# All modulation sums on VectorE, plain additions for the squares, and loads in long runs, in a decoder layer

## The chip, the core and the metric

The kernel runs on one core of one Trainium2 chip. Its time is device microseconds from the start to the end of one execution; several executions are timed, and one more is recorded by the hardware profiler. TensorE (PE) multiplies matrices at a granted clock of 1.2 or 2.4 GHz, VectorE (DVE) and GpSimd (POOL) work element by element, ScalarE (ACT) applies functions and scales, and SyncE (SP) issues the loads.

## The reference: what is computed

A decoder layer on x of 512 tokens by 2048 channels, all in float32:

```
mod = silu(c) @ w_mod + b_mod            # 2048 x 12288; six rows: sh1 sc1 g1 sh2 sc2 g2
h   = rms_norm(x, ln1_g) * (1 + sc1) + sh1
x   = x + g1 * hybrid_mixer(h)           # w_in (2048 x 3920), w_q_up, two attentions, w_out
h   = rms_norm(x, ln2_g) * (1 + sc2) + sh2
x   = x + g2 * hierarchical_moe(h)       # 32 experts, two per token, three matrices each
```

The mixer has eight heads of sparse attention (an indexer scores the keys, the best 128 are kept) and eight of stick-breaking attention. Of the modulation, c is one vector: silu(c) @ w_mod is a sum of 2048 rows of w_mod, each times one number.

## The kernel before

The program is written out in one order by hand; each engine takes its instructions in that order. All large tiles live in one pool of 23 slots of 8 KB per partition. SyncE issues the loads in the order of a list `items`, three or six items ahead of their use, and a load waits for a free slot.

**Phase one** runs in these stages (times of the profile before). *Start* (0 to 44 us): x arrives transposed in four blocks of 512 channels; ScalarE squares a block, VectorE sums it over its four rows of a partition (line 424, a reduction with a strided view), TensorE sums over the partitions, and `rstd` makes 1/rms. `times_rb` multiplies x by it: the first half of block 0 on VectorE, blocks 2 and 3 on GpSimd (line 430). Then come the tables for the position bias and the masks (lines 442 to 446). *Pieces* (44 to 199): the modulation of h is needed 256 channels at a time. For each of eight pieces `prepare(d)` makes shift and scale, and `piece(d)` projects with the columns of group A and of the first keys (B2). The work of `prepare(d+1)` is interleaved with `piece(d)`. The scale (and in piece 0 the shift too) is summed by TensorE; the shift of the other pieces is summed by `gemv`, 16 calls a piece. *B0 to Q3* (199 to about 350), *Q0, Q1, B1, B3* (to about 520) and *B5* (to 647) are projections of 512 columns in halves; every weight is split by `w_chunk` into a high part (ScalarE) and a low part (line 394, VectorE, or GpSimd from Q0 to B3), since a product takes three matmuls of the parts. Between the matmuls the two attentions are threaded in by `lanes`, four queues of generators that advance at hand-set rates. *O0 to O5* (647 to 897): the output projection in 32 halves; `add_up` multiplies the result by g1 (VectorE) and adds it to x (line 1025, GpSimd for all but the last segment).

The other four rows of the modulation (sc2, g1, sh2, g2; 64 items, 16 chunks of 2048 columns each) are spread among the weights of the later stages: `PRE = 3` first, then `MODS` says how many go into each of the six segments of `SEGS`. A chunk is one call of

```
def gemv(acc, w, s, cut, first):
    lo, hi = slice(0, cut), slice(cut, acc.shape[-1])
    if first:
        V.tensor_scalar(acc[:, lo], w[:, lo], s, None, op0=OP.mult)
        act(acc[:, hi], w[:, hi], AF.Identity, scale=s)
    else:
        V.scalar_tensor_tensor(acc[:, lo], w[:, lo], s, acc[:, lo], op0=OP.mult, op1=OP.add)
        act(w[:, hi], w[:, hi], AF.Identity, scale=s)
        G.tensor_tensor(acc[:, hi], acc[:, hi], w[:, hi], op=OP.add)
```

so VectorE (line 280) takes the columns below `cut` and ScalarE and GpSimd (line 282) the rest: 96 of 256 in the pieces, and of 2048 1280 for sc2 and sh2, 1536 for g1, 768 for g2.

**The experts** (from about 924 us): after a short routing, sixteen pairs of experts, 24 loads of 1 MB each pair, in order; the loads run as far ahead as free slots allow, and the first of them are asked for at the end of phase one.

Of the kernel before, what the change touches and what calls it, by code (L numbers as in the profile page):

```python
# [41 lines left out]
MODS = (5, 7, 4, 11, 4, 30)  # L42
# [4 lines left out]
SHARE = 6  # L47
CUT = (1280, 1280, 1536, 768)
# [29 lines left out]
def tile_hybrid_layer(ctx: ExitStack, tc, A, out, dbg=None):  # L78
    nc = tc.nc
    x, xT, w_mod, w_in, w_q_up, rel_bias, w_out = (  # L80
        A[k] for k in ("x", "xT", "w_mod", "w_in", "w_q_up", "rel_bias", "w_out"))
# [191 lines left out]
    def gemv(acc, w, s, cut, first):  # L273

        lo, hi = slice(0, cut), slice(cut, acc.shape[-1])
        if first:
            V.tensor_scalar(acc[:, lo], w[:, lo], s, None, op0=OP.mult)
            act(acc[:, hi], w[:, hi], AF.Identity, scale=s)
        else:
            V.scalar_tensor_tensor(acc[:, lo], w[:, lo], s, acc[:, lo], op0=OP.mult, op1=OP.add)  # L280
            act(w[:, hi], w[:, hi], AF.Identity, scale=s)
            G.tensor_tensor(acc[:, hi], acc[:, hi], w[:, hi], op=OP.add)  # L282

    def mod_chunk(v, c, q, lag):

        w = raw.pop(("m", v, c, q))
        if c is None:
# [5 lines left out]
            gemv(accs[v], w, sil[:, q:q + 1], CUTS[v], q == 0 and v not in (G1, G2))  # L293
# [8 lines left out]
        for i in range(r):  # L302
# [4 lines left out]
            else:  # L307
                gemv(acc, w[:, i], s, n * SHARE // 16, q == 0 and i == 0)
# [103 lines left out]


# [6 lines left out]
    for c in range(4):  # L420
# [17 lines left out]
    pb = bank("at", "b31")  # L438
    mm(pb[:8, :384], relb, ohd, True, True)
    brow = k2([8, 384], "brow")  # L440
    b31 = sm.tile([8, 1], F32, name="b31")
    V.tensor_copy(b31, pb[:8, 0:1])
    V.tensor_scalar(brow, pb[:8, :384], b31, None, op0=OP.subtract)
    V.tensor_copy(identb, ident)
    V.tensor_scalar(smaskb, ustrict, -NEG, NEG, op0=OP.mult, op1=OP.add)
    V.tensor_scalar(negU, ustrict, -1.0, None, op0=OP.add)
    dram = ctx.enter_context(tc.tile_pool(name="dram", bufs=1, space=bass.MemoryType.DRAM))
    bd = dram.tile([8, 384], F32, name="bd")
    G.dma_start(bd, brow)
# [527 lines left out]
    def main_o(c, q, h, start, stop):  # L977
# [9 lines left out]
        for t in range(4):  # L987
# [568 lines left out]
```

## Time and profile before

| | |
|---|---|
| runs, median of 3 | 1900.78 us (1898.29 to 1902.36) |
| profiled execution, its own time | 1895.36 us |
| its span, first to last instruction | 1893.6 us |
| busy: PE, DVE, ACT, POOL | 1740.0, 973.5, 601.5, 396.2 us |
| mean granted TensorE clock | 0.981 of 2.4 GHz |
| read from HBM | 583.64 MB |

Busy time is summed over the whole span. A matmul's record is longer than its share of PE, so that the PE can be busy throughout and still not at its peak; a wait shorter than that overlap does not show as idle time. The granted clock is a mean over a stretch: 0.5 would be 1.2 GHz throughout.

### The profile page before, as it was taken

The numbers are of one execution on the slowest core, as the hardware profiler recorded it, in microseconds if no ns is written. First come the engines' busy times: TensorE is split into PE (matmuls) and PEld (weight loads), VectorE is DVE, ScalarE is ACT, GpSimd is POOL, SyncE is SP. The second block draws the span as 40 slices with busy tenths as digits, with TensorE's granted clock in tenths as the row PEclk, the third lists the DMA queues.
The fourth block names the chain that finished last, engine by engine and source line by source line (L and its number), as shares of the span: only waits on it lengthen the run. The fifth ranks groups of instructions, "written<-read, shape, count | busy, mean of one in ns | idle before, by whom it ended". The sixth has DMA issues, their size and how long they took to land.

```text
span 1893.6 us, 21355 instructions
## 1 busy us (share of the span) xinstructions
PE 1740.0 (92%) x8097; PEld 976.8 (52%) x8097; DVE 973.5 (51%) x1486; ACT 601.5 (32%) x1136; POOL 396.2 (21%) x311
## 2 busy tenths in 40 slices
PE   4999999998999998899899999999999999999997
PEld 1777777765677676787334333333333333333333
DVE  6888722488855668768334334342433243333325
ACT  3645444554556543443222110111012111211010
POOL 3534311333437326656100000000000000000000
PEclk9999999999999998999999999999999999999999
DMA  9878322323226657768899999999999999999997
GB/s 349 285 263 300 123 79 94 133 90 111 90 89 224 227 178 267 267 245 354 359 418 420 419 420 418 420 419 419 419 420 419 420 419 420 419 420 419 419 413 275
DMA packets 136634, 585.09 MB, mean 309 GB/s; under 512 B 10866, under 2 KB 43802, under 8 KB 79270
## 3 DMA queue, kind: packets, MB, share of 16 engines
q1 hardware_dynamic: 132240, 569.09, 76.6%
q0 software_dynamic: 4288, 14.60, 2.1%
q8 instruction: 65, 1.06, 0.2%
q14 instruction: 41, 0.34, 0.0%
HBM read 583.64 MB, written 8.40 MB: 313 GB/s over the span
## 4 chain that ended last, share of the span: by engine, by line
DMA 39%; PE 20%; DVE 6%; issue 4%; ACT 2%; POOL 1%; SPq 0%; DVEq 0%; POOLq 0%; ACTq 0%
DMA w_u<-in_w_up 15%; DMA w_g<-in_w_gate 12%; DMA w_d<-in_w_down 12%; PE O L103 5%; PE y L103 3%; PE u L103 3%; PE g L103 2%; PE B L103 2%; DVE hl L394 1%; PE cb L103 1%; DVE accv L280 1%; DVE x L1288 1%; PE z L103 1%; PE ga L1252 1%; DMA xg<-x1d,gi 1%
## 5 line engine op out<-in xcount | busy, mean ns | idle before, releaser
L103 PE MATMUL u<-w_u,xe 128*64 128x512 f32 x1024 | 265.8, 605 | 24.4 <-DMA w_u<-in_w_up 23.7
L103 PE MATMUL g<-w_g,xe 128*64 128x512 f32 x1024 | 240.9, 596 | 18.4 <-DMA w_g<-in_w_gate 17.4
L1288 DVE TENSOR_TENSOR x<-cb,x 128x512 f32<-128x512 f32 x256 | 157.3, 682 | 186.7 <-PE cb L103 186.7
L103 PE MATMUL y<-w_d,uT 128*64 128x512 f32 x1024 | 236.9, 600 | 0.7 <-ACT uT L100 0.7
L282 POOL TENSOR_TENSOR accv<-accv,w_m_None 128x768 f32<-128x768 f32 (+2 forms) x62 | 153.0, 2468 | 210.6 <-ACT w_m_None L100 124.0
L1230 POOL DMA_INDIRECT xg<-x1d,gi x15 | 15.2, 1016 | 816.4 <-DVE t L1233 654.9
L103 PEld LDWEIGHTS u<-w_u,xe 128*64 128x64 f32 x1024 | 78.2, 138 | 201.5 <-issue 138.1
L103 PEld LDWEIGHTS g<-w_g,xe 128*64 128x64 f32 x1024 | 76.3, 137 | 170.5 <-issue 129.3
L1278 DVE SCALAR_TENSOR_TENSOR yt<-y,gs,accv 128x512 f32<-128x512 f32 x64 | 47.8, 747 | 200.5 <-PE y L103 200.5
L280 DVE SCALAR_TENSOR_TENSOR accv<-w_m_None,sil,accv 128x1280 f32<-128x1280 f32 (+2 forms) x62 | 132.6, 2138 | 6.2 <-issue 5.5
L100 ACT ACTIVATE xe<-ga,modc 128x128 f32<-128x128 f32 x254 | 94.1, 463 | 128.6 <-PE y L103 88.4
L103 PEld LDWEIGHTS y<-w_d,uT 128*64 128x64 f32 x1024 | 66.6, 136 | 116.1 <-issue 106.7
L100 ACT ACTIVATE uT<-uT 128x512 f32<-128x512 f32 x16 | 9.6, 600 | 343.4 <-PE uT L1329 343.4
L103 PE MATMUL cb<-yH,oT 128*128 128x512 f32 x256 | 107.8, 421 | 0.9 <-DVE x L1288 0.9
L100 ACT ACTIVATE yH<-yt 128x512 fp32r<-128x512 f32 x64 | 40.3, 630 | 204.5 <-DVE yt L1278 121.4
L103 PE MATMUL cb<-yL,oT 128*128 128x512 f32 x256 | 101.1, 395 | 0.0
L1280 DVE TENSOR_TENSOR yL<-yt,yH 128x512 fp32r<-128x512 f32 x64 | 44.3, 693 | 110.3 <-PE g L103 63.2
L394 DVE TENSOR_TENSOR hl<-w_O,hl 128x1024 fp32r<-128x1024 f32 x32 | 67.8, 2123 | 40.1 <-ACT hl L100 31.2
L282 POOL TENSOR_TENSOR acc<-acc,w_m 128x160 f32<-128x160 f32 x105 | 61.3, 584 | 70.1 <-ACT w_m L100 62.4
L103 PEld LDWEIGHTS cb<-yH,oT 128*128 128x128 f32 x256 | 48.0, 188 | 49.6 <-issue 38.6
L1252 PEld LDWEIGHTS ga<-cst,xg 128*128 128x128 f32 x252 | 35.2, 209 | 61.8 <-issue 41.0
L1323 DVE TENSOR_TENSOR u<-sg,u 128x512 f32<-128x512 f32 x16 | 11.0, 689 | 105.4 <-PE u L103 105.4
(435 smaller groups left out, 3171.5 us busy)
## 6 DMA issues: line engine op xcount, KB each, us to landing
w_g<-in_w_gate SPq DMA_DIRECT2D x128, 1024.0 KB, 19.9
w_u<-in_w_up SPq DMA_DIRECT2D x128, 1024.0 KB, 21.2
w_d<-in_w_down SPq DMA_DIRECT2D x128, 1024.0 KB, 19.9
w_m_None<-in_w_mod SPq DMA_DIRECT2D x64, 1024.0 KB, 5.0
w_m<-in_w_mod SPq DMA_DIRECT2D x32, 1024.0 KB, 11.0
w_B<-in_w_in SPq DMA_DIRECT2D x48, 512.0 KB, 4.7
w_O<-in_w_out SPq DMA_DIRECT2D x16, 1024.0 KB, 5.9
w_A<-in_w_in SPq DMA_DIRECT2D x8, 848.0 KB, 11.7
```

What stands on the lines that cost most here:

```text
L100: return SC.activation(o, i, f, **kw)
L103: return T.matmul(o, l, r, start=start, stop=stop, skip_group_check=skip)
L280: V.scalar_tensor_tensor(acc[:, lo], w[:, lo], s, acc[:, lo], op0=OP.mult, op1=OP.add)
L282: G.tensor_tensor(acc[:, hi], acc[:, hi], w[:, hi], op=OP.add)
L394: low_eng[0].tensor_tensor(t[:, 1], s, t[:, 0].bitcast(F32), op=OP.subtract)
L1230: G.indirect_dma_start(xs, None, x1d[:, :], bass.IndirectOffsetOnAxis(ap=gi[:, 0:1], axis=0), bounds_check=S - 1, oob_is_err=False)
L1252: T.transpose(pb[:, 128 * j:128 * j + 128], xs[:, 512 * c:512 * c + 512].rearrange("p (k j) -> p j k", j=4)[:, j], ident)
L1278: V.scalar_tensor_tensor(yt, y, g, rowv[G2][:, cs], op0=OP.mult, op1=OP.mult)
L1280: V.tensor_tensor(yL[:, cs], yt, yH[:, cs].bitcast(F32), op=OP.subtract)
L1288: return lambda: V.tensor_tensor(acc[q][:, t], pb, acc[q][:, t], op=OP.add)
L1323: V.tensor_tensor(u, sg, pb, op=OP.mult)
```

## The change

`gemv` loses its cut: one VectorE instruction takes all columns, and neither ScalarE nor GpSimd has a part. `times_rb` runs on VectorE for all blocks: half of block 0 at once, its other half before piece 0, and blocks 1, 2 and 3 after the pieces 0, 2 and 4. The squares of a block are summed by two additions. The masks and the bias row, with their matmul and a store, go ahead of the squares. The four chunks of piece 0's modulation are loaded two ahead of the first weights and two behind, not all behind. `MODS` is new, and `add_up` works on VectorE alone. On the host, the weights of phase one (the first two rows of w_mod, w_in, w_q_up, w_out) and x are laid out so that a load reads one run of 4 to 8 KB for each partition, where it read runs of 1 to 4 KB; the bytes loaded are the same.

```diff
-MODS = (5, 7, 4, 11, 4, 30)
+MODS = (20, 2, 6, 12, 4, 17)
-SHARE = 6
-CUT = (1280, 1280, 1536, 768)
...
             o, n, r = PIECES[c]
-            return w_mod_v[:, r * q:r * q + r, v * D + o:v * D + o + n], [P, r, n]
+            return A["w_m1"][c, v, q].rearrange("p (r n) -> p r n", r=r), [P, r, n]
...
-            return w_in_v[c][:, h, :, 0:NA], [P, 2, NA]
+            return A["w_a"][c, h].rearrange("p (j n) -> p j n", j=2), [P, 2, NA]
...
-            return w_in_v[c][..., BCOL + 512 * n:BCOL + 512 * (n + 1)], [P, 2, 2, 512]
+            return A["w_b"][n, c].rearrange("e p (j n) -> p e j n", j=2), [P, 2, 2, 512]
...
-            return w_o_v[:, 4 * q:4 * q + 4, 512 * c:512 * (c + 1)], [P, 4, 512]
+            return A["w_o"][c, q].rearrange("p (j n) -> p j n", j=4), [P, 4, 512]
...
-        k = len(mod) // 2 if d else 0
+        k = len(mod) // 2
         items += mod[:k] + wa + mod[k:] + wb
...
-    def gemv(acc, w, s, cut, first):
+    def gemv(acc, w, s, first):
         if first:
-            V.tensor_scalar(acc[:, lo], w[:, lo], s, None, op0=OP.mult)
-            act(acc[:, hi], w[:, hi], AF.Identity, scale=s)
+            V.tensor_scalar(acc, w, s, None, op0=OP.mult)
         else:
-            V.scalar_tensor_tensor(acc[:, lo], w[:, lo], s, acc[:, lo], op0=OP.mult, op1=OP.add)
-            act(w[:, hi], w[:, hi], AF.Identity, scale=s)
-            G.tensor_tensor(acc[:, hi], acc[:, hi], w[:, hi], op=OP.add)
+            V.scalar_tensor_tensor(acc, w, s, acc, op0=OP.mult, op1=OP.add)
...
-        V.tensor_reduce(sr, sq.rearrange("p j t -> p t j"), axis=AX.X, op=OP.add)
+        V.tensor_tensor(sq[:, 0:2], sq[:, 0:2], sq[:, 2:4], op=OP.add)
+        V.tensor_tensor(sr, sq[:, 0], sq[:, 1], op=OP.add)
         mm(pss, ones, sr, c == 0, c == 3)
...
     times_rb(0, range(2), V)
-    for c in (2, 3):
-        times_rb(c, range(4), G)
...
     times_rb(0, range(2, 4), V)
-    times_rb(1, range(4), V)
     for d in range(len(PIECES)):
...
+        if d in (0, 2, 4):
+            times_rb(d // 2 + 1, range(4), V)
...
-        eng.tensor_tensor(x1[c][:, t], x1[c][:, t], tmp, op=OP.add)
+        V.tensor_tensor(x1[c][:, t], x1[c][:, t], tmp, op=OP.add)
```

## Rows read from the trace of the kernel before

**Rows 1.** The page's chain that ended last, shares of the span by line.
```profile
DMA w_u<-in_w_up 15%; DMA w_g<-in_w_gate 12%; DMA w_d<-in_w_down 12%; PE O L103 5%; PE y L103 3%; PE u L103 3%; PE g L103 2%; PE B L103 2%; DVE hl L394 1%; PE cb L103 1%; DVE accv L280 1%; DVE x L1288 1%; PE z L103 1%; PE ga L1252 1%; DMA xg<-x1d,gi 1%
```

**Rows 2.** Windows cut at the stages; columns as in the heading line.
```profile
core 0: us, PE busy (x) PEld busy (x) DVE busy (x) ACT busy (x) POOL busy (x), PEclk, DMA share, GB/s
0.00:44.00 44.00, 18.07 (x79) 5.57 (x79) 30.09 (x28) 14.29 (x14) 14.91 (x16) 0.94 1.01 349
44.00:199.00 155.00, 146.01 (x974) 114.19 (x975) 137.04 (x232) 89.43 (x182) 69.08 (x109) 0.98 0.81 274
199.00:387.00 188.00, 184.03 (x804) 137.44 (x803) 75.78 (x92) 89.32 (x148) 47.27 (x38) 1.00 0.30 101
387.00:520.00 133.00, 119.61 (x548) 82.80 (x547) 115.32 (x240) 69.70 (x150) 45.95 (x22) 0.94 0.31 103
520.00:647.00 127.00, 120.45 (x573) 89.35 (x571) 76.11 (x80) 75.75 (x138) 61.26 (x41) 0.99 0.45 163
647.00:720.00 73.00, 65.47 (x263) 48.24 (x262) 48.60 (x46) 32.38 (x48) 27.14 (x19) 0.99 0.54 194
720.00:897.00 177.00, 162.42 (x894) 135.79 (x894) 135.92 (x82) 70.16 (x96) 110.80 (x51) 0.94 0.79 292
897.00:924.00 27.00, 18.14 (x98) 11.10 (x99) 13.87 (x67) 5.62 (x16) 2.11 (x2) 0.87 0.83 341
924.00:1893.00 969.00, 905.77 (x3876) 352.30 (x3872) 340.73 (x623) 154.90 (x350) 17.65 (x17) 0.99 1.00 411
```

**Rows 3.** What PE waited for from 44 to 199 us: total, times, longest.
```profile
PE B L103 <- DVE attA L484: 6.7, 6, 1.3
PE sh L103 <- DVE acc L280: 2.3, 1, 2.3
```

**Rows 4.** What PE waited for from 720 to 897 us.
```profile
PE O L103 <- DVE hl L394: 16.0, 4, 6.2
```

**Rows 5.** Timeline of the start: start, us, engine, line, instruction.
```profile
9.27 14.38 DVE L424 TENSOR_REDUCE sqr<-xsq 128x512 f32<-128x2048 f32 x4 [5.52 <-ACT xsq L100]
...
15.20 1.91 ACT L100 ACTIVATE xsq<-xt 128x2048 f32<-128x2048 f32 x1 [0.59 <-DMA xt<-in_xT]
...
23.71 2.08 PE L103 MATMUL xss<-sqr,one 128*128 128x512 f32 x2 [1.46 <-DVE sqr L424]
...
27.08 3.64 PE L103 MATMUL md<-w_m,sil 128*32 128x256 f32 x32
...
43.94 0.79 PE L103 MATMUL cq<-h0H,waH 128*128 128x512 f32 x1 [7.43 <-ACT h0H L100]
```

**Rows 6.** Timeline of VectorE: single modulation sums.
```profile
343.21 1.54 DVE L280 SCALAR_TENSOR_TENSOR accv<-w_m_None,sil,accv 128x1280 f32<-128x1280 f32 x1
...
865.70 3.67 DVE L280 SCALAR_TENSOR_TENSOR accv<-w_m_None,sil,accv 128x768 f32<-128x768 f32 x1
...
880.68 1.01 DVE L280 SCALAR_TENSOR_TENSOR accv<-w_m_None,sil,accv 128x768 f32<-128x768 f32 x1
```

**Rows 7.** VectorE's groups by shape from 44 to 199 us.
```profile
L280 DVE SCALAR_TENSOR_TENSOR acc<-w_m,sil,acc 128x96 f32<-128x96 f32 x105 | 54.5, 519 | 3.7
```

**Rows 8.** Line 394's instructions: least, median and largest ns.
```profile
L394 DVE TENSOR_TENSOR hl<-w_O,hl x32: 1211/2076/3960, 647.0 to 881.6; 128x1024 fp32r<-128x1024 f32 x32
...
L394 POOL TENSOR_TENSOR hl<-w_B,hl x17: 2365/2389/3900, 384.1 to 569.3; 128x1024 fp32r<-128x1024 f32 x17
```

**Rows 9.** Line 1025's instructions: least, median and largest ns.
```profile
L1025 DVE TENSOR_TENSOR x<-x,mix x4: 691/692/693, 888.5 to 895.0; 128x512 f32<-128x512 f32 x4
```

**Rows 10.** A window while x arrives; columns as in rows 2.
```profile
10.00:15.00 5.00, 2.01 (x2) 0.50 (x2) 5.00 (x2) 3.82 (x2) 0.00 (x0) 1.00 1.02 405
```

**Rows 11.** VectorE's groups by shape from 387 to 520 us.
```profile
L280 DVE SCALAR_TENSOR_TENSOR accv<-w_m_None,sil,accv 128x1280 f32<-128x1280 f32 x6 | 11.8, 1973 | 0.0
```

**Rows 12.** VectorE's groups by shape from 720 to 897 us.
```profile
L280 DVE SCALAR_TENSOR_TENSOR accv<-w_m_None,sil,accv 128x768 f32<-128x768 f32 x16 | 35.4, 2210 | 5.6 <-issue 5.5
L280 DVE SCALAR_TENSOR_TENSOR accv<-w_m_None,sil,accv 128x1280 f32<-128x1280 f32 x13 | 30.2, 2321 | 0.1
```

**Rows 13.** SyncE's queue from 866 us: the first expert load.
```profile
869.83 4.65 SPq L256 DMA_DIRECT2D w_g<-in_w_gate  x4
```

More of the change, by code (lines that the diff above doesn't have):

```diff
@@ L79, in tile_hybrid_layer @@
     nc = tc.nc
-    x, xT, w_mod, w_in, w_q_up, rel_bias, w_out = (
-        A[k] for k in ("x", "xT", "w_mod", "w_in", "w_q_up", "rel_bias", "w_out"))
+    xT, w_mod, rel_bias = (A[k] for k in ("xT", "w_mod", "rel_bias"))
     w_gate, w_up, w_down = A["w_gate"], A["w_up"], A["w_down"]
@@ L292, in mod_chunk @@
                     G.dma_start(accs[v][0:1], A["b_gate"][int(v == G2):int(v == G2) + 1])
-            gemv(accs[v], w, sil[:, q:q + 1], CUTS[v], q == 0 and v not in (G1, G2))
+            gemv(accs[v], w, sil[:, q:q + 1], q == 0 and v not in (G1, G2))
             if q == 15:
@@ L307, in mod_chunk @@
             else:
-                gemv(acc, w[:, i], s, n * SHARE // 16, q == 0 and i == 0)
+                gemv(acc, w[:, i], s, q == 0 and i == 0)
     def first_cols(c):
@@ L411, in advance @@
         load_to(n_done + AHEAD)
+    V.tensor_copy(identb, ident)
+    V.tensor_scalar(smaskb, ustrict, -NEG, NEG, op0=OP.mult, op1=OP.add)
+    V.tensor_scalar(negU, ustrict, -1.0, None, op0=OP.add)
+    pb = bank("at", "b31")
+    mm(pb[:8, :384], relb, ohd, True, True)
+    brow = k2([8, 384], "brow")
+    b31 = sm.tile([8, 1], F32, name="b31")
+    V.tensor_copy(b31, pb[:8, 0:1])
+    V.tensor_scalar(brow, pb[:8, :384], b31, None, op0=OP.subtract)
+    dram = ctx.enter_context(tc.tile_pool(name="dram", bufs=1, space=bass.MemoryType.DRAM))
+    bd = dram.tile([8, 384], F32, name="bd")
+    G.dma_start(bd, brow)
     rb = sm.tile([P, S], F32, name="rb", tag="rb", bufs=2)
@@ L432, in tile_hybrid_layer @@
     times_rb(0, range(2), V)
-    for c in (2, 3):
-        times_rb(c, range(4), G)
[L438 to L449, printed above, removed]
     tb = []
@@ L982, in main_o @@
             xc = slot([P, 4, 512], name=f"x1_{c}")
-            Q.dma_start(xc, x_v[:, :, 512 * c:512 * c + 512])
+            Q.dma_start(xc, A["x"][c].rearrange("p (t d) -> p t d", t=4))
             x1.append(xc)
@@ L995, in main_o @@
             if (c, q, h) == (3, 3, 1):
-                add_up(c, t, pm, V)
+                add_up(c, t, pm)
                 keep(c, t)
@@ L1013, in main_o @@
                 for t in range(4):
-                    add_up(c, t, pm, G)
+                    add_up(c, t, pm)
                 if q == 3:
@@ L1532, in _prepare @@
     cst, ohd, flip = _constants()
+    w_in = f("w_in")[0]
     a = {
-        "x": f("x").reshape(512, 2048), "xT": f("x").reshape(512, 2048).T, "w_mod": f("w_mod")[0],
-        "w_in": f("w_in")[0], "w_q_up": f("w_q_up")[0], "rel_bias": f("rel_bias"),
-        "w_out": f("w_out")[0], "w_gate": f("w_gate")[0], "w_up": f("w_up")[0], "w_down": f("w_down")[0],
+        "x": f("x").reshape(4, 128, 4, 512).transpose(2, 1, 0, 3).reshape(4, 128, 2048),
+        "xT": f("x").reshape(512, 2048).T, "w_mod": f("w_mod")[0],
+        "w_m1": f("w_mod")[0, :, :4096].reshape(128, 2, 8, 2, 8, 256).transpose(4, 3, 1, 0, 2, 5).reshape(8, 2, 2, 128, 2048),
+        "w_a": w_in[:, :NA].reshape(4, 2, 128, 2 * NA),
+        "w_b": w_in[:, NA:].reshape(4, 2, 128, 2, 6, 512).transpose(4, 0, 1, 2, 3, 5).reshape(6, 4, 2, 128, 1024),
+        "w_q": f("w_q_up")[0].reshape(4, 128, 4, 512).transpose(2, 1, 0, 3).reshape(4, 128, 2048),
+        "w_o": f("w_out")[0].reshape(4, 4, 128, 4, 512).transpose(3, 0, 2, 1, 4).reshape(4, 4, 128, 2048),
+        "rel_bias": f("rel_bias"), "w_gate": f("w_gate")[0], "w_up": f("w_up")[0], "w_down": f("w_down")[0],
         "router": fold(np.concatenate([f("router_g")[0], f("router_e")[0]], axis=1)), "vecs": vecs, "b_gate": bm[[2, 5]], "cst": cst, "ohd": ohd, "flip": flip,
```

11 lines of the change are left out of this document (2 added, 9 removed).

## The prediction

> **What bounds the kernel now.** First the chain that ended last [rows 1]: the loads of the experts' three matrices hold 15 + 12 + 12 = 39% of the span in it. Next the windows, cut at the stages [rows 2]: from 924 to 1893 us the loads move 411 GB/s at a DMA share of 1.00. So the expert part is a load stream of fixed length, and what comes before matters only through the time at which that stream can start. Before 897 us the loads are not the limit, except in the first 44 us (share 1.01). PE is: it is busy 184.0 of the 188 us from 199 to 387. So the change can win only where PE waits or is slowed before 897 us. That room, from rows 2 (window minus PE busy, plus what the clock costs: one minus the granted clock, times the window) is: 44 to 199, 9.0 + 3.1; 199 to 387, 4.0; 387 to 520, 13.4 + 8.0; 520 to 647, 6.5 + 1.3; 647 to 720, 7.5 + 0.7; 720 to 897, 14.6 + 10.6. The view of PE's waits names the culprits: in 44 to 199 VectorE's additions and sums [rows 3], in 720 to 897 VectorE's halves of the output weights, 16.0 us in four waits [rows 4]. And PE has no projection matmul to do before 43.94 us [rows 5].
>
> **Price of one instruction.** A modulation sum alone costs VectorE 1.54 us for 1280 columns and 1.01 us for 768 [rows 6], so 1.04 ns a column: 2048 columns are 1.54 + 768 × 0.00104 = 2.34 us, and 256 columns 1.01 − 512 × 0.00104 = 0.48 us (estimates from these two rows). Beside GpSimd the same 768 columns took 3.67 us [rows 6], and the 96-column sums average 519 ns [rows 7], more than 256 columns alone would. The halves of the output weights go from 1.21 us at best to 2.08 in the median [rows 8]. So with GpSimd's share moved onto VectorE, VectorE's total becomes about equal, not larger.
>
> **The start.** The last square ends at 15.20 + 1.91 = 17.1 us, the last reduction at 9.27 + 14.38 = 23.65, and the last sum matmul starts at 23.71 [rows 5]. Two plain additions, 1024 and 512 wide, cost 1.21 [rows 8] + 0.69 [rows 9] = 1.9 us, so that matmul starts at 19.0: 4.7 us sooner. The masks, now ahead of the squares, wait for small constants; VectorE has nothing to do before 9.27 us, which hides them. Were the constants as late as the last square, the masks' 4 us (estimate: five small instructions under 1 us each) would go in front of the additions; I price them at nothing. PE then runs the shift sums from 21.1 to 24.7 (3.64 us [rows 5]), a turn of 1 us, and the scale sums to 29.4. Before, the same order ended at 35.5, and another 8.4 us passed to the first projection matmul, with VectorE in a weight half and in tiny additions beside GpSimd's x products. Without those I estimate that tail as copy 0.4, turn 0.5, three small operations 0.5, scale 0.8, cast 0.6: 2.9 us. First projection matmul at 29.4 + 2.9 = 32.3, **11.5 us** sooner. Do the loads keep up? It needs 9.7 MB (x 4.2, constants 0.4, first weights 0.9, four sums 4.2); about 5.0 MB are in at 15 us. At the 349 GB/s of the first 44 us [rows 2], mostly runs of 1 KB, the rest is there at 28.5; at the 405 of x's longer runs [rows 10] at 26.6. The last scale sums start at 27.6. So the new layout is worth about 1 us here, and nothing in the pieces, which load at 274 GB/s [rows 2]. Bounds for the start: 4.7 (the squares alone) to 13.
>
> **The pieces (44 to 199).** PE waits about 1.1 us in each of six pieces, and 2.3 in the first [rows 3]. VectorE's sums of one piece go from 16 × 0.52 = 8.3 to 16 × 0.48 = 7.7 us; with its other work freed of GpSimd I take 1.4 us less in all. But the x products of the next 512 channels (4 × 0.69 = 2.8 us) now stand in front of the sums in pieces 1, 3 and 5: there VectorE is 1.4 us later than before and the wait grows from 1.1 to 2.5; in pieces 2, 4 and 6 it goes; the first loses its 2.3. Sum: −2.3 − 3 × 1.1 + 3 × 1.4 = −1.4; with less slow clock at the beginning **2 us** gained (bounds: 3 lost, 9 gained).
>
> **The middle.** Twenty sums now lie in 199 to 350 where five lay: 15 × 2.34 = 35 us more on a VectorE that is busy 76 of 188 [rows 2], hidden by PE's projections. Each may delay a half a little: I take 3 us lost, against 2 gained at the bias table, whose flip matrix is asked for once GpSimd's additions before it are done: **−1**. In 387 to 520, where VectorE is busy 115 of 133, eight sums of 2.34 stand for seven of about 2.0 [rows 11], 5 us more; GpSimd's sums no longer stand in VectorE's way there, for which I take 6 back: **+1**. In 520 to 647 twelve for eleven, **+1**. Bounds of the three: 15 lost, 25 gained.
>
> **The output projection.** 647 to 720 keeps four sums; the normalisation that ends in it loses GpSimd's additions as neighbours, they cost VectorE 0.69 each [rows 9]: **+4** of the room of 8. In 720 to 897 the sums fall from 30 to 17: 40 us in place of 66 [rows 12]; 24 halves cost 29 us at 1.21 in place of 50 at 2.08; sixteen gated additions in two steps 22. VectorE is left with about 95 of some 155 us instead of 136 of 177. The four waits for halves should go, and with them most of the slow clock of that stretch: **+20** of the 25 (bounds 8 and 25).
>
> **Sum.** 11.5 + 2 − 1 + 1 + 1 + 4 + 20 = 38.5 us. The expert stream begins with a load at 869.83 us [rows 13], asked for three items ahead of the projections' end; with a shorter tail it gains a little less, but in 897 to 924 the share is 0.83 [rows 2], which takes some of that up: I charge 1.5. The profiled execution took 1895.4 us; 1895.4 − 37 = 1858. It lies 5.4 under the runs' median of 1900.8, so against the runs: **1863 us**.
>
> **A rule against it.** Rows 6 show GpSimd and VectorE stretching each other. GpSimd keeps weight halves, 2.39 us each in the median [rows 8], in the stretch from 350 to 570, and the stick additions. The Trainium skill (SBUF — State Buffer, "Who interferes with whom") says that a VectorE instruction with two SBUF inputs and a GpSimd one that reads SBUF exclude each other for the whole instruction. The trace agrees in kind: 3.67 us are far more than a shared rate would make of 1.01. By that rule a longer sum means a longer block on both sides; what it would cost here is rival (c).
>
> **Rivals.**
> (a) All the room is won: 11.5 + 12.1 + 4 + 21.4 + 7.8 + 8.2 + 25.2 = 90, so about 1811. For it: the waits named have VectorE as their releaser. Against: in 387 to 520 its load does not fall. Chance 0.15.
> (b) The wait moves to 199 to 350. In 720 to 897, at 1.25 sums a half, PE lost 16.0 us over 24 halves [rows 4], 0.67 each; at one sum a half over 20 halves that is 13 us: 1876. Against: VectorE was busy 77% there and will be at some 60% here. Chance 0.16.
> (c) GpSimd's remaining halves and the longer sums block each other from 387 to 520: eight sums, each lengthened by one half of 2.39, are 19 us on the busiest VectorE: 1882. Against: GpSimd's own sums, which met them before, are gone. Chance 0.12.
> (d) The other side: in 199 to 350 the weight loads come late, since every second item is now a sum and only three items are loaded ahead. Twenty halves in 150 us are 7.5 us each; three items are a half and a half, 11 us, plus the half that is split ahead. A stall above 37 / 20 = 1.9 us a half decides for slower; at 3 us it is 1863 + 60 = 1923. Against: the DMA share there is 0.30 [rows 2], and 15 MB more at 400 GB/s add 37 of 188 us, 0.2. Chance 0.09.
>
> **Numbers.** The forecast 1863 (its own range 1845 to 1872) has 0.48, the rivals 0.15, 0.16, 0.12, 0.09. Leaving out half of (a) and all of (d) gives the range 1830 to 1886. A difference under 0.2% (3.8 us) can't be told from none. Faster: 0.48 + 0.15 + 0.16 + 0.11 = 0.90; same 0.03; slower 0.07, mostly (d).
>
> **What would show it.** First projection matmul near 32 us; no wait of PE for VectorE's halves in the last stage before the experts; sums of 2048 columns at 2.3 us each; the first expert load near 833 us, and the expert part as long as before. Wrong would be: waits for weight halves between 199 and 350, a start later than 38 us, or projections that end earlier without an earlier first expert load.

## The result and the profile after

| | before | after |
|---|---|---|
| runs, median of 4 | 1900.62 us (1898.29 to 1902.36) | 1875.8 us (1875.28 to 1876.9) |
| profiled execution, its own time | 1895.36 us | 1876.25 us |
| its span | 1893.6 us | 1874.4 us |
| busy: PE, DVE, ACT, POOL | 1740.0, 973.5, 601.5, 396.2 us | 1735.2, 938.9, 507.6, 153.2 us |

The ratio is 0.9877 (0.9863 to 0.989): the kernel is 1.2% faster, 24.8 us between the medians and 19.1 between the two profiled executions, on which all the sums below are made. (The kernel before ran 2.9 us faster in its profiled execution than in the fastest of its timed runs, which is most of the difference of the two figures.) A gain of 37 us was forecast: the direction is right and 1875.8 lies in the range of 1830 to 1886, but half of the gain is missing from the profile.

The chain that ended last, by line:
```profile
DMA w_u<-in_w_up 15%; DMA w_g<-in_w_gate 12%; DMA w_d<-in_w_down 12%; PE O L100 8%; PE B L100 7%; PE y L100 3%; PE u L100 3%; PE Q L100 2%; PE g L100 2%; PE z L100 2%; DVE accv L269 2%; DVE acc L269 1%; PE cb L100 1%; DVE sel L722 1%; DMA w_m<-in_w_m 1%
```
It answers to [rows 1]. The experts' loads hold the same 39%; in what stands before them PE's projections grew (`O` from 5 to 8%, `B` from 2 to 7%), and VectorE's halves are no longer listed.

Windows, cut where PE's work stands at the stages' boundaries (271 and 331 are added cuts inside B0 to Q3):
```profile
core 0: us, PE busy (x) PEld busy (x) DVE busy (x) ACT busy (x) POOL busy (x), PEclk, DMA share, GB/s
0.00:32.40 32.40, 14.90 (x78) 4.74 (x78) 15.91 (x31) 14.18 (x14) 2.51 (x8) 0.89 0.96 378
32.40:190.60 158.20, 149.54 (x976) 116.79 (x976) 136.51 (x239) 50.44 (x66) 6.72 (x3) 0.96 0.75 296
190.60:271.00 80.40, 77.35 (x327) 59.79 (x326) 54.93 (x54) 32.70 (x52) 8.92 (x10) 0.98 0.58 208
271.00:331.00 60.00, 49.41 (x304) 35.93 (x303) 22.29 (x23) 15.60 (x25) 5.95 (x6) 0.91 0.39 137
331.00:398.00 67.00, 66.78 (x307) 48.13 (x306) 28.57 (x45) 36.73 (x69) 20.16 (x15) 1.00 0.29 98
398.00:527.60 129.60, 114.95 (x487) 80.22 (x486) 114.24 (x232) 62.83 (x142) 32.81 (x14) 0.96 0.26 90
...
720.00:879.70 159.70, 154.33 (x890) 130.73 (x890) 87.47 (x81) 39.88 (x69) 6.83 (x9) 0.99 0.70 264
...
905.00:1874.00 969.00, 905.75 (x3870) 351.55 (x3866) 340.65 (x623) 153.32 (x347) 17.59 (x17) 0.99 1.00 411
```
They answer to [rows 2]. The expert part is 969 us at 411 GB/s, as before to the digit. The stage to look at is 271 to 331: PE idles 10.6 of 60 us, where it was idle for 4.0 us in all of 199 to 387 [rows 2], and in that stretch VectorE too is busy for only 22.29 us, ScalarE for 15.60. All are waiting for something.

To see where the time went, take the start of the same projection matmul in two timelines and subtract. Counted are the matmuls that write `cq`, `B`, `Q` and `O`, 2304 in every kernel, in order of time. The table, worked out from the timelines, holds microseconds earlier than before; the other columns are kernels of the next section.

| matmul, its time before | after | old_mods | held_slot | twelve | shared_sums | best4 |
|---|---|---|---|---|---|---|
| 1st, 43.94 | 11.5 | 12.6 | 11.2 | 12.7 | 12.5 | 10.6 |
| 384th, 198.88 (end of the pieces) | 8.7 | 9.2 | 7.2 | 9.5 | 4.2 | 10.1 |
| 672nd, 286.43 | 7.0 | 12.4 | 10.3 | 11.6 | 2.9 | 13.3 |
| 768th, 313.93 | -8.5 | 12.3 | 4.7 | 4.8 | 2.9 | 13.3 |
| 960th, 386.53 | -10.0 | 12.3 | 4.7 | 4.1 | 2.9 | 10.1 |
| 1248th, 527.19 | -6.0 | 10.9 | 1.5 | 14.7 | -0.5 | 15.8 |
| 1536th, 643.83 | -5.1 | 15.2 | 5.9 | 19.1 | -1.2 | 18.1 |
| 2304th, 893.72 (the last) | 16.8 | 38.6 | 28.7 | 44.1 | -0.9 | 42.0 |

Each column is one execution, and two executions of one kernel differ by some us: the 1st matmul, up to which old_mods, held_slot, twelve, shared_sums and best4 do the same work as after, starts between 10.6 and 12.7 us early.

The start came out as forecast. Timeline of the start:
```profile
16.19 1.91 ACT L97 ACTIVATE xsq<-xt 128x2048 f32<-128x2048 f32 x1 [0.76 <-DMA xt<-in_xT]
...
18.14 1.23 DVE L426 TENSOR_TENSOR xsq<-xsq 128x1024 f32<-128x1024 f32 x1 [0.71 <-ACT xsq L97]
...
19.47 0.69 DVE L427 TENSOR_TENSOR sqr<-xsq 128x512 f32<-128x512 f32 x1
...
20.21 2.08 PE L100 MATMUL xss<-sqr,one 128*128 128x512 f32 x2 [1.61 <-DVE sqr L427]
...
32.44 0.50 PE L100 MATMUL cq<-h0H,waH 128*128 128x512 f32 x1 [2.23 <-ACT h0H L97]
```
They answer to [rows 5]: the last sum matmul starts 2.1 us after the last square, the two additions last 1.23 and 0.69, and the first projection matmul is at 32.44 where 32.3 was forecast.

The tail too. PE's waits from 720 to 880 us, total, times, longest:
```profile
PE router L100 <- DVE router L963: 3.4, 1, 3.4
PE O L100 <- DVE mix L1013: 1.0, 1, 1.0
PE O L100 <- DVE hl L381: 0.8, 1, 0.8
```
Of the 16.0 us for halves [rows 4] 0.8 are left. The durations behind it, least, median and largest ns (line 269 is the sum, 381 the half):
```profile
L269 DVE SCALAR_TENSOR_TENSOR acc<-w_m,sil,acc x105: 483/485/491, 37.5 to 165.0; 128x256 f32<-128x256 f32 x105
L269 DVE SCALAR_TENSOR_TENSOR accv<-w_m_None,sil,accv x62: 2330/2344/3815, 177.8 to 852.5; 128x2048 f32<-128x2048 f32 x62
...
L381 DVE TENSOR_TENSOR hl<-w_O,hl x32: 1215/1222/1482, 650.9 to 851.3; 128x1024 fp32r<-128x1024 f32 x32
```
The prices 0.48 and 2.34 us for the sums were right, and the halves of the output weights went from a median of 2.08 [rows 8] to 1.22.

What was lost, from 190 to 331 us, stands in the waits; ScalarE's helper is line 97, its `hl` is the high half of a weight:
```profile
ACT hl L97 <- DVE accv L269: 29.0, 7, 9.4
...
ACT hl L97 <- PE B L100: 11.0, 3, 8.3
ACT hl L97 <- PE md L100: 10.5, 1, 10.5
...
PE z L100 <- DVE st L803: 6.4, 2, 3.8
ACT hl L97 <- PE pob L100: 4.7, 1, 4.7
```
A high half reads only a loaded weight. It has no data from a modulation sum (`accv`), from a projection's matmul (`B`, or the attention's `pob`) or from the matmuls that turn a finished modulation row into columns (`md`). What it does need is a slot of the pool for its result, and what it waits for is the last user of the tile that had the slot before. The timeline of all engines shows what stands behind it:
```profile
278.13 0.62 ACT L97 ACTIVATE st<-st,one 128x384 f32<-128x384 f32 x1
...
281.63 19.79 SPq L247 DMA_DIRECT2D w_m_None<-in_w_mod  x2
...
287.04 1.06 ACT L97 ACTIVATE hl<-w_B 128x1024 fp32r<-128x1024 f32 x1 [8.29 <-PE B L100]
288.00 0.85 ACT L97 ACTIVATE st<-z 128x384 f32<-128x384 f32 x2
...
290.79 1.19 PE L100 MATMUL z<-st,mone 128*128 128x256 f32 x2 [3.79 <-DVE st L803]
...
297.10 2.35 DVE L269 SCALAR_TENSOR_TENSOR accv<-w_m_None,sil,accv 128x2048 f32<-128x2048 f32 x1 [6.46 <-DMA accv<-in_b_gate]
299.49 1.06 ACT L97 ACTIVATE hl<-w_B 128x1024 fp32r<-128x1024 f32 x1 [9.44 <-DVE accv L269]
300.45 0.96 ACT L97 ACTIVATE st<-z 128x384 f32<-128x384 f32 x2
```
ScalarE stops for 8.29 us at the high half. The next instructions in its order are those of the stick attention (`st<-z`); they come 0.96 us after the half starts, VectorE's `st` after them, and PE, which has the attention's matmul `z` next in its order, has been idle for 3.79 us by then. The two load issues from 281.63 us, spread over 19.79 us, point to the same shortage at SyncE.

### The profile page after: what moved, and what is told of

The parts are those of the page before. It is cut to its first block, busy times and chain, and to the rows that moved or that the text cites. A ratio compares the mean times of both kernels' runs of the same rounds, so it can differ in the third digit from the quotient of the medians.

```text
span 1874.4 us, 20840 instructions
## 1 busy us (share of the span) xinstructions
PE 1735.2 (93%) x8097; PEld 975.6 (52%) x8097; DVE 938.9 (50%) x1518; ACT 507.6 (27%) x960; POOL 153.2 (8%) x116
## 4 chain that ended last, share of the span: by engine, by line
DMA 41%; PE 36%; DVE 14%; issue 4%; ACT 4%; POOL 1%; SPq 0%; DVEq 0%; ACTq 0%; POOLq 0%
DMA w_u<-in_w_up 15%; DMA w_g<-in_w_gate 12%; DMA w_d<-in_w_down 12%; PE O L100 8%; PE B L100 7%; PE y L100 3%; PE u L100 3%; PE Q L100 2%; PE g L100 2%; PE z L100 2%; DVE accv L269 2%; DVE acc L269 1%; PE cb L100 1%; DVE sel L722 1%; DMA w_m<-in_w_m 1%
## 5 line engine op out<-in xcount | busy, mean ns | idle before, releaser
L269 DVE SCALAR_TENSOR_TENSOR accv<-w_m_None,sil,accv 128x2048 f32<-128x2048 f32 x62 | 150.4, 2426 | 6.7 <-DMA accv<-in_b_gate 6.5
L1219 POOL DMA_INDIRECT xg<-x1d,gi x15 | 15.2, 1014 | 818.7 <-DVE t L1222 597.2
L97 ACT ACTIVATE hl<-w_B 128x1024 fp32r<-128x1024 f32 x48 | 50.5, 1052 | 54.9 <-DVE accv L269 29.5
L381 DVE TENSOR_TENSOR hl<-w_O,hl 128x1024 fp32r<-128x1024 f32 x32 | 39.2, 1229 | 43.6 <-ACT hl L97 28.3
L381 POOL TENSOR_TENSOR hl<-w_B,hl 128x1024 fp32r<-128x1024 f32 x17 | 47.9, 2817 | 142.6 <-ACT hl L97 112.3
## 6 DMA issues: line engine op xcount, KB each, us to landing
w_u<-in_w_up SPq DMA_DIRECT2D x128, 1024.0 KB, 21.2
```

The source lines that it names most:

```text
L97: return SC.activation(o, i, f, **kw)
L269: V.scalar_tensor_tensor(acc, w, s, acc, op0=OP.mult, op1=OP.add)
L381: low_eng[0].tensor_tensor(t[:, 1], s, t[:, 0].bitcast(F32), op=OP.subtract)
L1219: G.indirect_dma_start(xs, None, x1d[:, :], bass.IndirectOffsetOnAxis(ap=gi[:, 0:1], axis=0), bounds_check=S - 1, oob_is_err=False)
```

## Experiments

Four theories stood for the 15 us lost between 271 and 331 us. **S**: the 23 slots run out, because a loaded chunk of 8 KB now stands beside every half; the high half waits for a slot and holds back ScalarE's queue. **V**: VectorE's twenty longer sums delay the halves, as rival (b) had it. **G**: the gates' bias row does it, since the first sum of g1 waits for a memset on GpSimd and a load, 6.46 us above. **L**: the loads come late, as in rival (d). Diffs are against the kernel after; times are medians, ratios are to the kernel before on the same chip.

| kernel | us (lowest to highest) | ratio (95%) |
|---|---|---|
| old_mods | 1859.6 (1858.55 to 1860.19) | 0.9793 (0.9777 to 0.9809) |
| ahead2 | 1874.21 (1869.88 to 1875.46) | 0.9866 (0.9848 to 0.9883) |
| no_gate_row | 1882.83 (1880.14 to 1885.09) | 0.992 (0.9904 to 0.9937) |
| twelve | 1854.68 (1851.05 to 1860.67) | 0.9778 (0.9757 to 0.98) |
| held_slot | 1865.52 (1862.62 to 1867.38) | 0.9821 (0.9806 to 0.9836) |
| shared_sums | 1898.14 (1893.24 to 1903.33) | 0.9995 (0.9984 to 1.0007) |
| old_squares | 1881.83 (1880.99 to 1887.29) | 0.992 (0.9901 to 0.9939) |
| old_layout | 1861.77 (1861.26 to 1866.32) | 0.9811 (0.9793 to 0.983) |
| spread_rb | 1877.04 (1870.18 to 1879.88) | 0.988 (0.9854 to 0.9906) |
| best2 | 1857.42 (1856.6 to 1859.7) | 0.9784 (0.9771 to 0.9798) |
| best3 | 1852.34 (1850.53 to 1853.78) | 0.9756 (0.9743 to 0.9769) |
| best4 | 1851.21 (1849.14 to 1853.91) | 0.9747 (0.9734 to 0.9761) |

### The respread undone: old_mods

```diff
-MODS = (20, 2, 6, 12, 4, 17)
+MODS = (5, 7, 4, 11, 4, 30)
```


> The changed kernel with the old spread of the sums (5, 7, 4, 11, 4, 30). Theory S (the 23 slots run out in 271 to 331 us, since one loaded chunk now stands beside every weight half): the idle and slow PE of that stretch (10.6 us idle, about 5 us of slow clock) goes; the output projection carries 30 sums of 2.34 us, 70 + 29 + 22 = 121 of some 160 us of VectorE, and loses at most 8 us of its gain; about 1868 us. Rival V (it is VectorE's long sums that delay PE, wherever they stand): the output projection loses most of its 19 us again; 1880 us or more.

Measured 1859.6, 16 us less than after. The windows and the first waits from 190 to 331 us:
```profile
190.00:271.00 81.00, 81.00 (x347) 62.39 (x346) 37.52 (x46) 33.15 (x53) 4.17 (x9) 1.00 0.30 103
271.00:331.00 60.00, 58.99 (x253) 44.34 (x251) 14.46 (x15) 27.57 (x44) 8.99 (x10) 1.00 0.26 91
```
```profile
ACT hl L97 <- DVE accv L269: 5.4, 2, 3.3
ACT hl L97 <- PE B L100: 3.1, 3, 1.1
```
So the respread alone made the loss. And it bought nothing: with thirty sums instead of seventeen in O2 to O5, the stretch from 641 us to the last matmul gains 38.6 − 15.2 = 23.4 us (last two rows of the table), against 16.8 + 5.1 = 21.9 after. The measurement is below what either theory gave, since the tail lost nothing. Whether the chunks' storage or their sums made the loss is not told by this run, as it takes both away.

### Fewer loads ahead: ahead2

```diff
+    AHEAD = 2
     steps("B0", 0.5)
...
+    AHEAD = 3
     low_eng[0] = G
```


> The changed kernel, but from B0 to Q3 loads are asked for two items ahead, not three; sums and their places are the same. Theory S (slots): one slot fewer is held by loaded data, so PE's idle time from 271 to 331 us falls from 10.6 to under 5 us; about 1868 us. Rival V (VectorE's sums): unchanged, 1876. Rival L (the loads come late): the waits for weight halves grow, over 20 us idle there, 1885 or more.

Measured 1874.21, hardly less than after. In the window from 271 to 331 us PE is busy 54.23 us, against 49.41 after, so its idle time falls from 10.6 to 5.8. Its row:
```profile
271.00:331.00 60.00, 54.23 (x333) 39.72 (x331) 22.98 (x25) 20.54 (x33) 8.55 (x8) 0.94 0.45 158
```
That a shorter lookahead helps here speaks for S and against L. But S had asked for under 5 us and a total of 1868, and got neither; the total is nearer to V's 1876, and by the ratios it can't be told from after. ScalarE's halves wait elsewhere instead: for `B` 24.2 us in four waits from 190 to 331 us, the longest 10.8.

### Without the gates' bias row: no_gate_row

The kernel leaves out the bias of the two gates.
```diff
-                if v in (G1, G2):
-                    G.memset(accs[v], 0.0)
-                    G.dma_start(accs[v][0:1], A["b_gate"][int(v == G2):int(v == G2) + 1])
-            gemv(accs[v], w, sil[:, q:q + 1], q == 0 and v not in (G1, G2))
+            gemv(accs[v], w, sil[:, q:q + 1], q == 0)
```


> The changed kernel with its new spread, but the gate accumulators (g1, g2) start with a plain product like the others: no GpSimd memset, no load of the bias row, no wait of VectorE for it. It leaves the gates' bias out. Theory G (the loss in 271 to 331 us comes from the start of g1's accumulator, which now falls among the stick additions: VectorE stood 6.5 us before that load): PE's idle time there falls from 10.6 to under 4 us; about 1866. Theory S (no free slot, whatever starts): it stays above 8 us; 1872 or more.

Measured 1882.83: slower than after, not faster. Its row of that window:
```profile
271.00:331.00 60.00, 47.82 (x287) 34.36 (x286) 20.28 (x22) 13.73 (x22) 3.84 (x4) 0.86 0.36 123
```
PE idles 12.2 us. The wait for the bias row was a consequence that happened to be in the same place: GpSimd's memset at 292.96 had stood behind the stick attention's additions, which were late already. G is out. Why this kernel is 7 us slower than after is not shown.

### Twelve chunks in the first segment: twelve

```diff
-MODS = (20, 2, 6, 12, 4, 17)
+MODS = (12, 0, 4, 11, 4, 30)
```


> The changed kernel with MODS (12, 0, 4, 11, 4, 30): against the old spread only seven chunks move from Q0, Q1 and B1 into the first segment, and g1's accumulator starts in the same place as with the old spread. Theory G (start of the gate accumulator): nothing is lost in the first segment, 1859 like the old spread. Theory S (loaded chunks hold the slots): about half of the 16 us is lost there, 1867.

Measured 1854.68. Its row of that window:
```profile
271.00:331.00 60.00, 54.71 (x224) 41.01 (x223) 16.50 (x13) 22.00 (x37) 6.63 (x8) 0.94 0.31 106
```
Both expected totals, 1859 and 1867, were missed. Twelve chunks idle PE for 5.3 us, between the 1.0 of five and the 10.6 of twenty, and the table shows 6.7 us lost between the 672nd and the 768th matmul (15.5 after). The wait of 8.3 us on `B` is there again, at 282.46 us, and PE's 3.8 on `st` with it. From the 960th to the 1248th matmul it wins 10.6 where old_mods loses 1.4: there the seven chunks of the second segment (Q0, Q1, B1) are gone, and best2, which has none there either, wins 11.8. This brings the total below both expectations; the prediction too had weighed longer sums against shorter ones there, and not a stretch without any. (The profiled execution of twelve is the fastest of its runs, 3.6 us under their median.)

### One slot fewer, and nothing else: held_slot

old_mods, and an empty tile that holds one slot of the pool through B4. No load and no sum is added, two memsets of one column on GpSimd take it and free it.
```diff
-MODS = (20, 2, 6, 12, 4, 17)
+MODS = (5, 7, 4, 11, 4, 30)
...
+    held = [slot([P, D], name=f"held{k}") for k in range(1)]
+    for t in held:
+        G.memset(t[:, 0:1], 0.0)
     steps("B4", RATES[0])
+    for t in held:
+        G.memset(t[:, 0:1], 1.0)
     steps("Q2", RATES[0])
```


> The changed kernel with the old spread of the sums and one slot of the pool held by an empty tile throughout B4: no more loads and no more sums than with the old spread. Theory S (free slots): the projections lose time there as they do with twenty chunks, 3 to 10 us between 199 and 331 us, ScalarE's high halves waiting for slots; 1863 to 1870. Rival V (VectorE's sums or the loads themselves are what delays): nothing is lost, 1859.6 within 2 us.

Measured 1865.52, 5.9 more than old_mods and within the expected 1863 to 1870; the ranges of the two kernels do not meet, the intervals of their ratios just touch. In the table it loses 5.6 us between the 672nd and the 768th matmul, where old_mods loses none. The window of 271 to 331, and the timeline:
```profile
271.00:331.00 60.00, 55.42 (x233) 41.78 (x232) 11.98 (x11) 23.01 (x38) 5.97 (x9) 0.97 0.25 88
```
```profile
283.68 1.06 ACT L97 ACTIVATE hl<-w_B 128x1024 fp32r<-128x1024 f32 x1 [8.29 <-PE B L100]
...
287.44 0.67 PE L100 MATMUL z<-st,mone 128*128 128x256 f32 x2 [3.79 <-DVE st L803]
...
289.09 0.10 POOL L928 MEMSET held<- 128x1 f32 x1
289.22 1.06 ACT L97 ACTIVATE hl<-w_B 128x1024 fp32r<-128x1024 f32 x1 [2.52 <-POOL held L928]
```
With VectorE at 11.98 us of 60, less than in any of the others, the loss is back, down to the same 8.29 and 3.79 us. The last line says it in one row: a high half of a weight waits 2.52 us for a memset of a tile with which it has nothing in common but the slot. So one slot fewer is enough for this loss, without one sum or load more: S is shown, and V is not needed for it.

How the 16 us of after divide is not shown. Its twenty chunks hold slots as loaded data, but they also bring the end of sc2 and the beginning of g1 into this stretch: 3 + 20 chunks are sixteen of sc2 and seven of g1, so that two accumulators of a slot each stand side by side. The wait of 10.5 us is for `md`, the last reader of sc2's accumulator, and the sum at 297.10 is the first of g1. In twelve, where g1 starts later, 6.7 us are lost where after loses 15.5. Nor does the trace list which slots are free at a moment: that they are short is read from the waits.

### Sums shared as before: shared_sums

old_mods, with the sums again cut among VectorE, ScalarE and GpSimd; all else as after.
```diff
-MODS = (20, 2, 6, 12, 4, 17)
+MODS = (5, 7, 4, 11, 4, 30)
...
+    CUTS = {SC2: 1280, SH2: 1280, G1: 1536, G2: 768}
...
+        lo, hi = slice(0, cut), slice(cut, acc.shape[-1])
...
+            V.scalar_tensor_tensor(acc[:, lo], w[:, lo], s, acc[:, lo], op0=OP.mult, op1=OP.add)
+            act(w[:, hi], w[:, hi], AF.Identity, scale=s)
+            G.tensor_tensor(acc[:, hi], acc[:, hi], w[:, hi], op=OP.add)
```


> The changed kernel with the old spread and the old sharing of the sums between VectorE, ScalarE and GpSimd. If GpSimd's share stretched VectorE and made the halves late, the output projection loses its 19 us again and the pieces and the middle some 3 to 6: about 1883 against 1859.6 with all sums on VectorE. Rival (the sharing was harmless, what helped in the output projection were the gated additions on VectorE): 1866 or less.

Measured 1898.14, no different from before (0.9984 to 1.0007), and 38.5 more than old_mods; 1883 was expected. All the other edits together are worth nothing without this one: the 12.5 us of the start are there in the table, and gone at the 1248th matmul. The costliest groups of the page show the exchange, here of shared_sums (busy us, mean ns, then idle before):
```profile
L275 POOL TENSOR_TENSOR accv<-accv,w_m_None 128x768 f32<-128x768 f32 (+2 forms) x62 | 153.8, 2481 | 249.4 <-ACT w_m_None L97 153.6
...
L273 DVE SCALAR_TENSOR_TENSOR accv<-w_m_None,sil,accv 128x1280 f32<-128x1280 f32 (+2 forms) x62 | 130.9, 2111 | 6.6 <-issue 5.1
```
and of old_mods:
```profile
L269 DVE SCALAR_TENSOR_TENSOR accv<-w_m_None,sil,accv 128x2048 f32<-128x2048 f32 x62 | 152.1, 2454 | 0.4
```
Giving 153.8 us of additions to GpSimd spared VectorE 21.2 us of these sums. And the halves of the output weights pay for it: 2.08 us in the median in shared_sums, 1.22 in old_mods and after. Least, median and largest ns in shared_sums:
```profile
L387 DVE TENSOR_TENSOR hl<-w_O,hl x32: 1210/2078/4293, 648.3 to 882.6; 128x1024 fp32r<-128x1024 f32 x32
```

### The squares by one reduction: old_squares

```diff
-        V.tensor_tensor(sq[:, 0:2], sq[:, 0:2], sq[:, 2:4], op=OP.add)
-        V.tensor_tensor(sr, sq[:, 0], sq[:, 1], op=OP.add)
+        V.tensor_reduce(sr, sq.rearrange("p j t -> p t j"), axis=AX.X, op=OP.add)
```


> The changed kernel with the strided reduction of the squares as before; masks stay ahead. If the last sum matmul waits for VectorE's last reduction (3.65 us against 1.9 us, and a backlog from the blocks before), the first projection matmul moves from 32.4 to about 37 us and the time by the same: 1880. Rival (the loads of the first sums are what the start waits for): under 2 us later, 1877.

Measured 1881.83, 6.0 more than after. In its timeline the last sum matmul starts at 24.63 us instead of 20.21, and the first projection matmul at 36.38 instead of 32.44. So 3.9 of the 11.5 us are the squares. The rest lies behind the sums over the partitions; no run divides it among the masks, the x products, the order of the loads and the layouts.

### The layouts as they were: old_layout

old_mods, with the loads read again through strided views (one line of six shown):
```diff
-            return A["w_b"][n, c].rearrange("e p (j n) -> p e j n", j=2), [P, 2, 2, 512]
+            return w_in_v[c][..., NA + 512 * n:NA + 512 * (n + 1)], [P, 2, 2, 512]
```


> The changed kernel with the old spread and the old layouts in memory (runs of 1 to 4 KB where the change has 4 to 8 KB). If only the first 32 us are bound by loads, the start comes 1 us later and nothing else: about 1861. Rival (the longer runs also shorten the tail, where 30 chunks and the weights load at 330 GB/s): 1866 or more.

Measured 1861.77, 2.2 more than old_mods and near the expected 1861. But the two ran on different chips, on which the kernel before differs by 2.1 us, and the intervals of their ratios overlap, so that no difference in the total is shown. The rate of the loads does differ: the window to the first projection matmul moves 346 GB/s instead of 378. That matmul is at 33.73 instead of 31.33 us; in the kernels with the new layouts and the same code up to there it starts between 31.3 and 33.3, so no more than one or two us can be put down to the layouts.

### The x products spread: spread_rb

Two of four products in each of six pieces, after the piece's own work, instead of four in front of every second piece:
```diff
+        if 0 < d < 7:
+            k = 2 * ((d + 1) % 2)
+            times_rb((d + 1) // 2, range(k, k + 2), V)
         yield
...
-        if d in (0, 2, 4):
-            times_rb(d // 2 + 1, range(4), V)
```


> The changed kernel with the x products of blocks 1 to 3 spread two a piece, behind the making of h, instead of four in front of the sums of pieces 1, 3 and 5. If these products in front of the sums cause the waits of 2.5 us in pieces 1, 3 and 5 and the slow clock behind them (7.8 us of waits, about 5 of clock), the pieces shorten by 6 to 9 us: about 1868. Rival (the waits only move to the next product): within 2 us of 1876.

Measured 1877.04, as after and as the rival had it. But the pieces end at 187.44 us instead of 190.14, where 6 to 9 us were expected. Against after it is 4.5 us ahead at the 768th matmul, 2.8 at the 960th and 0.9 at the last. After's timeline shows what the pieces had lost:
```profile
65.99 0.31 PE L100 MATMUL sh<-one,acc 128*32 128x1 f32 x16 [1.17 <-DVE attA L473]
...
68.33 0.79 PE L100 MATMUL B<-h0H,hl 128*128 128x512 f32 x1 [1.59 <-DVE attA L473]
...
69.34 1.05 PE L100 MATMUL B<-h0H,hl 128*128 128x512 f32 x2
...
74.29 0.62 PE L100 MATMUL B<-h0H,hl 128*128 128x512 f32 x2
```
Two matmuls take 1.05 us at 69.34 and 0.62 at 74.29: behind the two waits PE ran for about six us, from 68.33 to 74, at the lower of its clocks (1.2 GHz). The windows of 60 to 80 us say it in one number, first after, then spread_rb, whose granted clock is 1.00:
```profile
60.00:80.00 20.00, 17.24 (x114) 13.36 (x107) 16.24 (x32) 5.62 (x7) 0.00 (x0) 0.83 0.76 313
```
```profile
60.00:80.00 20.00, 19.20 (x139) 14.64 (x141) 17.82 (x35) 5.63 (x7) 0.00 (x0) 1.00 0.76 309
```
The prediction had the waits, and not the clock behind them.

### Three spreads tried for speed: best2, best3, best4

All three have spread_rb's edit and a spread of their own. The first:
```diff
-MODS = (20, 2, 6, 12, 4, 17)
+MODS = (8, 0, 5, 14, 4, 30)
```


> The changed kernel with MODS (8, 0, 5, 14, 4, 30) and the x products spread behind the making of h. Theory S: eight chunks in the first segment cost at most 3 us there (five cost none, twelve cost 8), the absence of sums in Q0, Q1 and B1 gives 8 to 10 as with twelve, the spread products some 3 in the pieces: about 1846. Rival (fourteen chunks in B5 use up the slots there): 1855.

Measured 1857.42, near the rival's 1855. PE is idle for 2.5 us from 271 to 331, but between the 672nd and the 768th matmul nothing is lost: it is 13.9 us earlier than before at both. The fourteen chunks in B5 bring the waits to that stage: 6.0 us for VectorE's `st` and 3.5 for a half between 520 and 640 us, and from the 1248th to the 1536th matmul it falls from 22.5 us earlier than before to 13.3.

The second, with the spread of twelve:
```diff
-MODS = (20, 2, 6, 12, 4, 17)
+MODS = (12, 0, 4, 11, 4, 30)
```


> The changed kernel with MODS (12, 0, 4, 11, 4, 30) and the x products spread behind the making of h. If the 3 us that the spread products won in the pieces are kept in the first segment: 1851 against 1854.7. Rival (the first segment waits for slots whose release is set elsewhere, and takes them back): 1855.

Measured 1852.34, where 1851 and the rival's 1855 were expected, with an interval that overlaps that of twelve: at the 768th matmul it is 2.2 us ahead of twelve, at the 960th 0.9 behind, so what the pieces win is lost again between.

The third:
```diff
-MODS = (20, 2, 6, 12, 4, 17)
+MODS = (8, 1, 7, 11, 4, 30)
```


> The changed kernel with MODS (8, 1, 7, 11, 4, 30) and the x products spread behind the making of h. With eight chunks the first segment lost nothing, with eleven B5 lost nothing, and with fourteen it lost 13 us. Theory S (a stage loses once its loaded chunks take the last free slots): eight here and eleven there keep both, about 1846, the fastest so far. Rival (eight chunks in B1 and B3 are as many as these can't hide either): 1853 or more.

Measured 1851.21, the lowest median here, with a ratio of 0.9747 (0.9734 to 0.9761), an interval that overlaps those of best3 and twelve: 24.6 us below the kernel after, and between the expected 1846 and the rival's 1853. From 271 to 331 us it has the row of best2, and from 720 to 850 PE is busy 129.24 of 130 us at a clock of 1.00. Where less than forecast came out, the table shows it: 3.2 us lost between the 768th and the 960th matmul. The trace has there a wait of PE of 2.2 us (`pob`, for ScalarE's `B`) and a granted clock of 0.91 from 300 to 320 us; why the wait stands there was not tried.

## Why the prediction was right and wrong

All on the profiled executions, in us gained, from the table; the last line closes the sum to the span.

| term | forecast | after | old_mods |
|---|---|---|---|
| start | +11.5 | +11.5 | +12.6 |
| pieces, 44 to 199 | +2 | −2.8 | −3.4 |
| 199 to 387 | −1 | −18.7 | +3.1 |
| 387 to 520 | +1 | +4.0 | −1.4 |
| 520 to 647 | +1 | +0.9 | +4.3 |
| 647 to 897 | +24 | +21.9 | +23.4 |
| handover to the experts | −1.5 | +2.4 | −2.8 |
| sum | 37 | 19.2 | 35.8 |

**The step that failed** is the middle: "hidden by PE's projections. Each may delay a half a little: I take 3 us lost". Twenty sums did hide behind PE's projections, as VectorE time; what they did not hide is the slot that each chunk holds from the issue of its load to the end of its sum. The step priced an instruction, and left out the storage. In place of 1 us, 18.7 were lost there, of which 15.5 lie between the 672nd and 768th matmul. At the bias table, too, the forecast's gain of 2 stayed out for want of a slot: GpSimd's `hank` load, after which the flip matrix is asked for, waited for a slot held by a half,
```profile
POOL hank L443 <- DVE hl L381: 3.6, 1, 3.6
```
and PE stood 3.1 us for the flip matrix, 3.0 before; in old_mods this wait is gone, and it gains 3.2 us from the 384th to the 672nd matmul. Held_slot shows the mechanism without one sum more, and old_mods shows the line at +3.1 and the sum at 35.8 with the chunks spread as before.

**The start** was right to 0.2 us (32.44 against 32.3), by its parts: additions 1.9, shift sums 3.64. Two of its small errors cancel: the last sum matmul was 1.2 us later than worked out and the scale sums were done in two times 1.07 us, with a wait for their load in between. The masks cost the last sum nothing, as priced. For the bound "the squares alone", 4.7, old_squares measured 3.9.

**The pieces** had the right waits, and the wrong sum. In pieces 1, 3 and 5 PE waits 2.76, 2.52 and 2.53 us, against the 2.5 forecast, and hardly in 2, 4 and 6. The forecast added 0.6 us (from 1.4 to 2) for less slow clock at the beginning, and the clock came out the other way: by its granted share the stage loses (1 − 0.96) × 158.2 = 6.3 us, against 3.1 before. Of that, about (1 − 0.83) × 20 = 3.4 us lie behind the first of these waits, and spread_rb, which breaks it up, won 2.7.

**The output projection** was right in size, and half wrong in its reason. The sums' move from 30 to 17 was counted among the causes; old_mods keeps thirty and loses nothing. The whole of it is that GpSimd no longer adds a part of the sums (shared_sums, with the gated additions on VectorE, gains 0.3 us in this stretch): the halves at 1.22 us instead of 2.08, and VectorE's sums alone.

**What the sums on one engine are worth** was not a term of its own, and by shared_sums it is 38.5 us, the whole of old_mods' gain. With the sums shared, the 12.5 us of the start are lost again, 8.4 of them in the pieces; whether the x products and the gated additions, now also on VectorE, are the reason, no run shows. The prediction weighed a rule of the Trainium skill (SBUF — State Buffer, "Who interferes with whom"), that an instruction of VectorE with two inputs from SBUF and one of GpSimd that reads SBUF exclude each other. It agrees with shared_sums and old_mods in kind: GpSimd's additions of 153.8 us spared VectorE only 21.2 of its sums. That the two stretch each other is more than [rows 6] show, which are VectorE's alone.

**The rivals.** (a) didn't come: of its 90 us the kernel after won 19.2 and old_mods 35.8. (b) named the right place and very nearly the time, 1876, and its mechanism is wrong: in the stretch that lost, VectorE is busy 37% (22.29 of 60), and held_slot has the loss at 20%. So its number is luck. It would have led to lighter sums, where fewer chunks in that stage were the cure (old_mods, twelve). (c) is out: 387 to 520 us gained 4.0, the GpSimd halves keep their median of 2.39 us (their mean rose from 2.60 to 2.82), and the 43 sums from 190 to 720 us average 2446 ns against a median of 2344, so 43 × 0.10 = 4.4 us of meeting, not 19. (d) priced the loads by their bandwidth, and saw the danger in three items being too few; in ahead2 two leave PE less idle from 271 to 331 us than three.

**The forecast's own signs.** "Waits for weight halves between 199 and 350" was the sign for wrong, and it is what the trace shows, only one engine further up: not PE waiting for VectorE's half, but ScalarE's half waiting for its slot. The first expert load is issued at 847.76 us, not 833, 22 us before that of [rows 13].

## What to carry to other kernels

When work is moved to another stage, price the buffer that its operand holds from the load's issue to its last reader, beside the instruction: count the slots in use in the stage that receives it, and look which engine's in-order queue stands behind the first instruction that asks for one. In a trace such a shortage looks like a dependence without sense: an instruction waits for one with which it shares no data, and its releaser is the last reader of a tile that is gone. And an element-by-element sum that is shared between VectorE and GpSimd should be tried on VectorE alone before it is rebalanced: here its neighbours' time came back with it, and the kernel was 38.5 us faster.

## What the runs showed of the hardware that was not expected

GpSimd's company cost VectorE more than its share of the work was worth: 62 sums of 768 to 1536 columns took 130.9 us beside GpSimd (shared_sums), 62 of 2048 took 152.1 alone (old_mods), 21.2 more; and 32 halves that had no part in it went from 2.08 to 1.22 us in the median, about 32 × 0.86 = 27 us less. Two waits of 1.17 and 1.59 us, 2.3 us apart, were followed by about six us at TensorE's lower clock, so that they cost about twice their length (2.76 us of waits, and half of the 5.7 us from 68.33 to 74.04).
